# An RWKV layer on one NeuronCore: shifted inputs from a scaled copy and the neighbours' sum, GpSimd's queue in the scan, and operands at 1.7 parts per stretch

## The chip, the core and the metric

The program runs on one NeuronCore of a Trainium2 chip. The metric is device time in microseconds (us). The engines are named as in the profile: PE is TensorE (PEld its weight loads), DVE is VectorE, ACT is ScalarE, POOL is GpSimd, SP is SyncE, which issues most of the DMAs.

## What is computed

The program is a chain of blocks over 512 tokens and, from the second half on, 256 context tokens, all at width 1024: hybrid layers, a gated unit, one RWKV layer, latent attention, and a gated unit again. Only the RWKV layer is touched. Its reference, cut to what matters:

```python
def center_shift(h):
    prev = jnp.pad(h[:, :-1], ((0, 0), (1, 0), (0, 0)))
    nxt = jnp.pad(h[:, 1:], ((0, 0), (0, 1), (0, 0)))
    return 0.5 * (prev + nxt) - h

def rwkv7_features(h, mu, w_in, ...):
    xx = center_shift(h)
    xs = h[:, :, None, :] + xx[:, :, None, :] * mu          # six shifted inputs
    rkvz = jnp.einsum('blcd,cde->blce', xs[:, :, :4], w_in)  # r, k, v, z
    ...                                                      # decay w and rate a from xs[4], xs[5]

def rwkv7_scan(state0, r, decay, k_dir, v, kk, a, emit):     # two directions, 16 heads of 64
    def step(S, inp):
        s_kk = jnp.einsum('nbhvk,nbhk->nbhv', S, kk_t)
        S = S * w_t - s_kk * (kk_t * a_t) + v_t * k_t
        y_t = jnp.einsum('nbhvk,nbhk->nbhv', S, r_t)
        return S, y_t

def rwkv7_output(y, r, k_dir, v, z, r_k, ln_gain, ln_bias, w_out):
    yn = head_norm(y) * ln_gain + ln_bias
    bonus = sum(r * k_dir * r_k) * v
    return ((yn + bonus) * silu(z)) @ w_out
```

The kernel computes the scan in chunks of 64 tokens (12 chunks, context and tokens together, in each direction). For each chunk it needs products within the chunk and the inverse of a unit triangular matrix.

## The kernel before, in words

Activations lie with features on partitions: 1024 features are eight tiles of 128, and a tile has 768 columns (512 tokens, 256 context). A float32 product is made of three: each operand is split into a high part (hi, a copy on ACT) and a low part (lo, a subtraction), and `mm3` multiplies hi by hi, lo by hi and hi by lo. Weights arrive raw by DMA (wraw), ACT makes whi, and DVE or POOL makes wlo.

**features()** makes the scan's inputs. `strips()` walks over the kinds in the order k, r, z, v. A kind has eight strips, a strip is 128 output features, and a strip has eight steps of 128 input features, each with three products of two pieces (512 and 256 columns). So a strip is 24 pairs of matmuls. After every two steps, `strips()` yields: that is a stretch, four to a strip. At a yield `features()` gives each of four side jobs its credit: `lora` 1.0 parts per stretch, `operands` OPS = 2.4, `by_tokens` 2.5, `first` 3.0; beside the first and last strip of a kind, only 0.4 of these. PE's order is fixed as written here (`in_order`); the orders of the other engines come from a scheduler, except in the opening, where those of DVE and POOL are fixed too.

The opening works on the eight input tiles in a pipeline: `hidden` (norm and modulation, L1360), `neighbours` (POOL adds the left and the right neighbour into xx), `difference` (DVE turns xx into half the sum minus h, L1372), `shifted` (DVE makes xs = xx times mu plus h in two pieces, L1383; ACT copies its high part, L1384; POOL or DVE makes its low part, L1385), and then the products of two strips of k. `shifted` is called for six inputs of eight tiles: k, r, z, v and the two of `lora`. The inputs of the next kind are made beside the last strip of a kind.

`operands(f)`, for each of eight feature tiles, has 17 parts: matmuls for decay and rate (L1603), transposes by matmul (L1264), a chain of some thirty elementwise operations with two scans (L1621 to L1664), which writes st_ar and st_bk, and for either direction `within`, the chunk products of st_ar and st_bk (L1679). `by_tokens(f)` turns v of one tile to token order once its strip and its operands are done. `feature_out` for strip f of v runs the side jobs until by_tokens has reached f - 2.

`first()` starts when v's inputs are ready. It computes inverse 0 on DVE: 31 columns of two operations each (L1819, L1821). It does `merge(0)`, which makes the chunk's whole inverse from its blocks, and waits until all eight operands are done. Then it starts inverse 1 on POOL, in whose queue two DMA issues and two memsets (L1812, L1813) stand ahead of the columns.

**scan()** has nine stages p. The lanes of stage p are the first six steps of tile p and the last six of tile p - 1; a step copies rh from PE's sums on DVE (L1892), multiplies it by the inverse (L1885), and goes on to the next state. Beside the lanes are woven: the products of coming groups, `merge(p+1)`, `inverse(p+2)` on POOL, and `output(p-2)`. An output ends so: ACT scales and shifts yacc (L1957), POOL adds the bonus (L1959), DVE multiplies by z (L1961), ACT makes yh and POOL yl, and the products with the output weights follow. `merge` also clears two quarters of its tile TT, on POOL (L1846).

Of the kernel before, what the change touches and what calls it, by code (L numbers as in the profile page):

```python
# [11 lines left out]
F32 = mybir.dt.float32  # L12
# [3 lines left out]
AF = mybir.ActivationFunctionType  # L16
ALU = mybir.AluOpType
# [4 lines left out]
KD = D // 128  # L22
# [1161 lines left out]
PACE = 0.4  # L1184
OPS = 2.4
WT = 3


class Rwkv:
# [92 lines left out]
    def params_with(self, kp):  # L1282
        net, nc = self.net, self.net.nc
        with net.psum(0, 2):
            P = self.params(kp)

        self.hb = kp.tile([128, 48], F32, name="hb")
        nc.vector.tensor_scalar(self.hb[:, 0:16], P["w0"], 0.5, None, ALU.mult)
        nc.vector.tensor_scalar(self.hb[:, 16:32], P["a0"], 0.5, None, ALU.mult)
        nc.vector.tensor_scalar(self.hb[:, 32:40], P["ka"], 0.5, None, ALU.mult)  # L1290
        nc.vector.tensor_scalar(self.hb[:, 40:48], P["ka"], -0.5, 1.0, ALU.mult, ALU.add)

        self.bones = kp.tile([128, 128], F32, name="bones")
        nc.gpsimd.memset(self.bones, 0.0)
        for e in range(2):
            nc.gpsimd.memset(self.bones[64 * e:64 * e + 64, 64 * e:64 * e + 64], 1.0)
        return P
# [69 lines left out]

    def difference(self, k):

        for src, _, n, t0 in self.hp:  # L1370
            xv = self.xx[k][:, t0:t0 + n]
            self.net.nc.vector.scalar_tensor_tensor(xv, xv, 0.5, src[k], ALU.mult, ALU.subtract)  # L1372

    def shifted(self, c, k, pool, tags, eng, late=False):

        nc, T = self.net.nc, S + C
        mu = self.P["mu"][:, c * 8 + k:c * 8 + k + 1]
        n = 9 if pool is self.xsp else 1
# [3 lines left out]
        for src, _, n, t0 in self.hp:  # L1382
            nc.vector.scalar_tensor_tensor(t[:, t0:t0 + n], self.xx[k][:, t0:t0 + n], mu, src[k], ALU.mult, ALU.add)  # L1383
        nc.scalar.copy(hi, t)  # L1384
# [30 lines left out]
    def strips(self):  # L1415
# [9 lines left out]
        with in_order(net.tc, nc.vector, nc.gpsimd):  # L1425
            for j in range(KD + 4):
                for at, part in enumerate((self.hidden, self.neighbours, self.difference)):
                    if 0 <= j - at < KD:
                        part(j - at)
                if 0 <= j - 3 < KD:  # L1430
                    x, l = prep(0, j - 3, True)
                    xs.append(x)
                    low.append(l)
                if j >= 4:
                    k = j - 4
                    low[k]()
# [38 lines left out]
    def first(self):  # L1475

        tc = self.net.tc
        while self.done["xs"] != "v":
            yield
        self.cur = cur = [{} for k in range(KD)]  # L1480
        X = [self.big(2), self.big(3)]
        cut = lambda t, a, n: t[:, a:a + n]
# [349 lines left out]
    def merge(self, k, cur, work, acc):  # L1832

        net, nc, ap = self.net, self.net.nc, self.ap
        mt = cur["mt"]
        TA = cur["TT"] = work("TT", [128, 2, NS, CH], 1, k)
        T12 = work("T12", [128, 2, 24, 32], 1)
        T1, M = T12[:, 0], T12[:, 1]
        TF = TA.rearrange("p d s t -> p (d s) t")
        for e in range(2):  # L1840
            nc.sync.dma_start(M[64 * e:64 * e + 32], self.mo[k][e])
            nc.sync.dma_start(T1[64 * e:64 * e + 32], self.blocks(mt[1], e, 0))
            for h in range(2):
                q = 64 * e + 32 * h
                nc.sync.dma_start(TF[q:q + 32, :, 32 * h:32 * h + 32], self.blocks(mt[0], e, h))
            nc.gpsimd.memset(TF[64 * e + 32:64 * e + 64, :, 0:32], 0.0)  # L1846
        for _ in range(8):
# [85 lines left out]
    def output(self, k, cur):  # L1933
# [24 lines left out]
        yield  # L1958
        nc.gpsimd.tensor_tensor(y, y, bonus, ALU.add)  # L1959
        yield  # L1960
# [3 lines left out]
        yl = ap.tile([128, T], F32R, tag="yl", name="yl", bufs=1)  # L1964
        net.split(yh, yl, y, nc.gpsimd)
        yield
        for f in range(KD):
            if f % 4 == 0:
                hi, lo = net.wtile([(0, net.I["rwkv_w_out_2"][0][rows, f * 128:f * 128 + 512])], 1, 512)
            a, b = net.acc(), net.acc()  # L1970
# [492 lines left out]
```

## Time and profile before

| What | Value |
|---|---|
| Median of three runs (lowest, highest) | 4227.73 us (4226.45, 4228.69) |
| Profiled execution: its own time, its span | 4218.81 us, 4216.9 us |
| PE, PEld, busy share of the span | 91%, 76% |
| DVE, ACT, POOL, busy share of the span | 58%, 37%, 31% |
| Mean DMA rate | 102 GB/s |

The RWKV layer lies between about 1990 and 3080 us of the span. Its stages, with PE's busy time in each:

| Stage, us of the span | Length | PE busy | DVE busy | POOL busy |
|---|---|---|---|---|
| Opening, 1994 to 2045 | 51 | 26.9 | 48.6 | 35.3 |
| Strips of k, 2045 to 2125 | 80 | 79.9 | 43.5 | 25.1 |
| Strips of r and z, operands, 2125 to 2425 | 300 | 230.5 | 211.1 | 158.6 |
| Strips of v, 2425 to 2540 | 115 | 102.7 | 53.1 | 90.1 |
| First part of the scan, 2540 to 2700 | 160 | 86.7 | 63.1 | 138.5 |
| Rest of the scan, 2700 to 3080 | 380 | 320.2 | 266.6 | 93.6 |

An engine's share over the whole span hides such stages; a stage is read by what PE waits for in it. In the rows below, a time in square brackets is the idle time ahead of an instruction, with the engine and tile whose end released it.

### The profile page before, as it was taken

Reading aid. Unit: us, or ns where it says so; the run is one execution under the profiler, and the core shown is the slowest. Engines: PE = TensorE matmul, PEld = TensorE weight load, DVE = VectorE, ACT = ScalarE, POOL = GpSimd, SP = SyncE. Lnnn points to the kernel's source line nnn. Section 1 sums busy time; section 2 is a strip of 40 time slices with the busy share of each in tenths; the row PEclk is TensorE's granted clock in tenths of the full one; section 3 lists DMA queues with packets and bytes.
Section 4 is the critical chain, followed back from the end, with each engine's and each line's share of the span. In section 5 each row is a group of like instructions: output and inputs, shape, how many; then the busy total and the mean of one; then the engine's idle time right before and its main releaser. Section 6 shows DMA issues by size and latency. Waiting matters only on the chain. (4 is left out here: it accounts for less than half of the span.)

```text
span 4216.9 us, 67232 instructions
## 1 busy us (share of the span) xinstructions
PE 3855.6 (91%) x26432; PEld 3192.2 (76%) x26432; DVE 2461.7 (58%) x4804; ACT 1545.2 (37%) x2945; POOL 1317.8 (31%) x1340
## 2 busy tenths in 40 slices
PE   8999999999999999998887797588789899998999
PEld 7867777787877788887766576477577788887887
DVE  7836445865554434444767644477643778883544
ACT  4243223334332422223454433244343455553222
POOL 3321111322111211113445578820121344442221
PEclk9999999999999999999899898799889999999999
DMA  3125543213364322222257866355223121221332
GB/s 92 51 79 162 175 132 90 61 56 100 103 202 158 102 65 61 60 61 78 70 158 202 226 166 156 91 128 124 79 61 114 51 61 52 61 77 62 93 91 85
DMA packets 599015, 431.72 MB, mean 102 GB/s; under 512 B 193436, under 2 KB 532140, under 8 KB 598700
## 3 DMA queue, kind: packets, MB, share of 16 engines
q1 hardware_dynamic: 593756, 414.97, 34.1%
q0 software_dynamic: 4944, 12.46, 1.2%
q8 instruction: 209, 3.42, 0.3%
q14 instruction: 106, 0.87, 0.1%
HBM read 354.46 MB, written 68.68 MB: 100 GB/s over the span
## 5 line engine op out<-in xcount | busy, mean ns | idle before, releaser
L138 ACT CAST whi<-wraw 128x1024 fp32r<-128x1024 f32 (+3 forms) x471 | 457.5, 972 | 1183.0 <-PE acc L160 971.4
L141 POOL TENSOR_TENSOR wlo<-wraw,whi 128x1024 fp32r<-128x1024 f32 (+2 forms) x205 | 426.9, 2083 | 1291.3 <-ACT whi L138 1182.1
L160 PE MATMUL acc<-hh,whi 128*128 128x512 f32 (+2 forms) x1776 | 625.2, 377 | 9.5 <-ACT hh L421 5.0
L160 PE MATMUL acc<-hl,whi 128*128 128x512 f32 (+2 forms) x1776 | 620.8, 374 | 2.5 <-DVE hl L422 2.5
L160 PE MATMUL acc<-hh,wlo 128*128 128x512 f32 (+2 forms) x1776 | 620.3, 374 | 2.0 <-DVE wlo L141 2.0
L141 DVE TENSOR_TENSOR wlo<-wraw,whi 128x1024 fp32r<-128x1024 f32 (+3 forms) x266 | 330.6, 1244 | 467.1 <-ACT whi L138 420.7
L160 PEld LDWEIGHTS acc<-hh,whi 128*128 128x128 f32 (+1 forms) x1776 | 314.7, 188 | 84.0 <-ACT whi L138 17.3
L160 PEld LDWEIGHTS acc<-hh,wlo 128*128 128x128 f32 (+1 forms) x1776 | 314.4, 187 | 63.4 <-DVE wlo L141 2.8
L160 PEld LDWEIGHTS acc<-hl,whi 128*128 128x128 f32 (+1 forms) x1776 | 314.6, 188 | 62.3 <-DVE hl L422 4.1
L160 PE MATMUL acc<-wlo,hh 128*128 128x256 f32 (+1 forms) x896 | 297.2, 332 | 6.5 <-DVE wlo L141 6.5
L160 PE MATMUL acc<-whi,hh 128*128 128x256 f32 (+1 forms) x896 | 298.1, 335 | 2.9 <-ACT hh L978 2.3
L160 PE MATMUL acc<-whi,hl 128*128 128x256 f32 (+1 forms) x896 | 293.4, 331 | 1.5 <-DVE hl L979 1.5
L999 DVE SCALAR_TENSOR_TENSOR xT<-acc,mod,xT 128x512 f32<-128x512 f32 x256 | 185.6, 746 | 139.6 <-PE acc L160 138.9
L160 PEld LDWEIGHTS acc<-wlo,hh 128*128 128x128 f32 x896 | 179.5, 201 | 20.4 <-DVE wlo L141 7.3
L160 PEld LDWEIGHTS acc<-whi,hh 128*128 128x128 f32 x896 | 179.4, 201 | 20.5 <-ACT hh L978 2.9
L160 PEld LDWEIGHTS acc<-whi,hl 128*128 128x128 f32 x896 | 178.4, 200 | 16.3 <-DVE hl L979 2.4
L160 PE MATMUL wide<-xsh,whi 128*128 128x512 f32 (+1 forms) x512 | 147.4, 371 | 16.5 <-ACT xsh L1384 16.5
L160 PE MATMUL wide<-xsl,whi 128*128 128x512 f32 (+1 forms) x512 | 142.0, 360 | 17.0 <-POOL xsl L1385 13.5
L160 PE MATMUL wide<-xsh,wlo 128*128 128x512 f32 (+1 forms) x512 | 140.0, 356 | 0.0
L160 PE MATMUL acc<-ffgh,whi 128*128 128x512 f32 x352 | 139.9, 400 | 0.0
L160 PE MATMUL acc<-ffgl,whi 128*128 128x512 f32 x352 | 138.4, 395 | 0.0
L160 PE MATMUL acc<-ffgh,wlo 128*128 128x512 f32 x352 | 138.3, 395 | 0.0
(625 smaller groups left out, 8754.9 us busy)
## 6 DMA issues: line engine op xcount, KB each, us to landing
ada_w<-in_ada_w SPq DMA_DIRECT2D x32, 1536.0 KB
wraw<-in_sgu_w_in SPq DMA_DIRECT2D x96, 512.0 KB
wraw<-in_w_up SPq DMA_DIRECT2D x88, 512.0 KB
wraw<-in_w_in SPq DMA_DIRECT2D x44, 512.0 KB
wraw<-in_w_down SPq DMA_DIRECT2D x32, 512.0 KB
wraw<-in_sgu_w_out SPq DMA_DIRECT2D x32, 512.0 KB
wraw<-in_rwkv_w_in SPq DMA_DIRECT2D x32, 512.0 KB
bk<-rw_bk SPq DMA_DIRECT2D x24, 512.0 KB
```

What stands on the lines that cost most here:

```text
L138: nc.scalar.copy(hi, raw)
L141: eng.tensor_tensor(lo, raw, hi.bitcast(F32), ALU.subtract)
L160: mm(out, lhsT=a, rhs=b[:, t0:t1], start=first and n == 0, stop=last and n == 2)
L999: nc.vector.scalar_tensor_tensor(dst[k], ps, m[:, 16 + k, j:j + 1], dst[k], ALU.mult, ALU.add)
```

## The change

Four edits, all in the RWKV layer.

1. The shifted input is written as (1 - mu) h plus mu/2 times the neighbours' sum. `difference` is gone; for each shifted input ACT makes two scaled copies of h (512 and 256 columns), and DVE adds the sum in one operation of 768 columns. Two tables of factors, mus, are made once. The opening's pipeline is one tile shorter.
2. OPS is 1.7 instead of 2.4.
3. In an output, the bonus add, and the low part yl, go from POOL to DVE, and so does wlo of the output weights, of which the third in turn was POOL's.
4. TT has three tiles that stay, instead of one for each merge from a pool, and they are cleared by DVE in the first three merges only.

The inverse itself is as it was; it stays on POOL.

```diff
-OPS = 2.4
+OPS = 1.7
...
+        self.mus = kp.tile([128, 2, 48], F32, name="mus", bufs=1)
+        nc.vector.tensor_scalar(self.mus[:, 0], P["mu"], -1.0, 1.0, ALU.mult, ALU.add)
+        nc.vector.tensor_scalar(self.mus[:, 1], P["mu"], 0.5, None, ALU.mult)
...
-    def difference(self, k):
-
-        for src, _, n, t0 in self.hp:
-            xv = self.xx[k][:, t0:t0 + n]
-            self.net.nc.vector.scalar_tensor_tensor(xv, xv, 0.5, src[k], ALU.mult, ALU.subtract)
...
         for src, _, n, t0 in self.hp:
-            nc.vector.scalar_tensor_tensor(t[:, t0:t0 + n], self.xx[k][:, t0:t0 + n], mu, src[k], ALU.mult, ALU.add)
+            nc.scalar.activation(t[:, t0:t0 + n], src[k], AF.Copy, scale=mu[:, 0])
+        nc.vector.scalar_tensor_tensor(t, self.xx[k], mu[:, 1], t, ALU.mult, ALU.add)
         nc.scalar.copy(hi, t)
...
-            for j in range(KD + 4):
-                for at, part in enumerate((self.hidden, self.neighbours, self.difference)):
+            for j in range(KD + 3):
+                for at, part in enumerate((self.hidden, self.neighbours)):
...
-        TA = cur["TT"] = work("TT", [128, 2, NS, CH], 1, k)
+
+        if k < 3:
+            self.tts.append(work("TT", [128, 2, NS, CH], 1, k))
+        TA = cur["TT"] = self.tts[k % 3]
...
-            nc.gpsimd.memset(TF[64 * e + 32:64 * e + 64, :, 0:32], 0.0)
+            if k < 3:
+                nc.vector.memset(TF[64 * e + 32:64 * e + 64, :, 0:32], 0.0)
...
-        nc.gpsimd.tensor_tensor(y, y, bonus, ALU.add)
+        nc.vector.tensor_tensor(y, y, bonus, ALU.add)
...
-        net.split(yh, yl, y, nc.gpsimd)
+        net.split(yh, yl, y)
...
-                hi, lo = net.wtile([(0, net.I["rwkv_w_out_2"][0][rows, f * 128:f * 128 + 512])], 1, 512)
+                hi, lo = net.wtile([(0, net.I["rwkv_w_out_2"][0][rows, f * 128:f * 128 + 512])], 1, 512, nc_lo=nc.vector)
```

How the order of instructions moves, at three places. A line number is that of the kernel the rows belong to.

DVE in the opening, two tiles of the pipeline. L1360 (L1364 after) is `hidden`, xx_16291 (xx_16294) the neighbours' sum, xT and cT the tiles of tokens and context. Before:

```order
L1360 SCALAR_TENSOR_TENSOR xT_81<-xT_81,mod_4351,aux 128x512
L1360 SCALAR_TENSOR_TENSOR cT_11756<-cT_11756,mod_4351,aux 128x256
L1372 SCALAR_TENSOR_TENSOR xx_16292<-xx_16292,xT_79 128x512
L1372 SCALAR_TENSOR_TENSOR xx_16292<-xx_16292,cT_11754 128x256
L1383 SCALAR_TENSOR_TENSOR xs<-xx_16291,col_rwkv,xT_78 128x512
L1383 SCALAR_TENSOR_TENSOR xs<-xx_16291,col_rwkv,cT_11753 128x256
```

After:

```order
L1382 SCALAR_TENSOR_TENSOR xs<-xx_16294,mus,xs 128x768
L1364 SCALAR_TENSOR_TENSOR xT_81<-xT_81,mod_4351,aux 128x512
L1364 SCALAR_TENSOR_TENSOR cT_11756<-cT_11756,mod_4351,aux 128x256
L1382 SCALAR_TENSOR_TENSOR xs<-xx_16295,mus,xs 128x768
L1364 SCALAR_TENSOR_TENSOR xT_82<-xT_82,mod_4351,aux 128x512
```

Four operations of DVE for a tile's shifted input have become one, which reads the scaled copy (xs) that ACT made.

PE at the last of the `within` products (L1679). Before, in strip 5 of z; wide_19399 is that strip's sum:

```order
L160 MATMUL wide_19399<-xsh_18370,wlo_19396 128x512
L160 MATMUL wide_19399<-xsh_18370,wlo_19396 128x256
L1679 MATMUL aux_19473<-st_ar_19450,st_bk_19451 64x64 [waits DVE_49]
L1679 MATMUL aux_19473<-st_ar_19450,st_bk_19451 64x64 x15
L1679 MATMUL aux_19491<-st_ar_19450,st_bk_19451 64x64 [waits Activation_49]
L1679 MATMUL aux_19491<-st_ar_19450,st_bk_19451 64x64 x7
L160 MATMUL wide_19399<-xsh_18383,whi_19395 128x512
```

After, in strip 4 of v; wide_20032 is its sum, L1553 belongs to `by_tokens`, L1870 to merge 0:

```order
L160 MATMUL wide_20032<-xsh_19285,wlo_20029 128x512
L160 MATMUL wide_20032<-xsh_19285,wlo_20029 128x256
L1679 MATMUL aux_20194<-st_ar_20122,st_bk_20123 64x64 [waits DVE_49,Activation_49]
L1679 MATMUL aux_20194<-st_ar_20122,st_bk_20123 64x64 x15
L1679 MATMUL aux_20212<-st_ar_20122,st_bk_20123 64x64 [waits Activation_49]
L1679 MATMUL aux_20212<-st_ar_20122,st_bk_20123 64x64 x7
L1553 MATMUL aux_20228<-vt_20048,back_19471 128x128 [waits PE_49,Activation_49]
L1870 MATMUL aux_20236<-xx3_19949,xx2_19948 32x32 [waits PE_49,Activation_49]
L160 MATMUL wide_20032<-xsh_19299,whi_20028 128x512
```

The last operand has moved by seven strips, past the change of kind, and now stands among the token passes and merge 0.

POOL at the first output of the scan, among the columns of an inverse. Before:

```order
L1819 TENSOR_TENSOR invP<-invA,invT 96x240
L1959 TENSOR_TENSOR yacc<-yacc,ld_b 128x768
L1821 TENSOR_TENSOR invT<-invT,invP 96x12x20
L1819 TENSOR_TENSOR invP<-invA,invT 96x231
L1821 TENSOR_TENSOR invT<-invT,invP 96x11x21
L178 TENSOR_TENSOR yl<-yacc,yh 128x768
```

And DVE at the same output after, where L1896 is the copy of rh, L1963 the bonus add, L1965 the multiplication by z:

```order
L1896 COPY rh<-aux 128x128 x2
L1959 TENSOR_TENSOR yacc<-yacc,acc 128x512
L1959 TENSOR_TENSOR yacc<-yacc,acc 128x256
L1902 COPY VU<-aux 64x2x64
L1963 TENSOR_TENSOR yacc<-yacc,ld_b 128x768
L1902 COPY VU<-aux 64x2x64
L1912 SCALAR_TENSOR_TENSOR st<-st,rw_ec,aux 128x64 x2
L1965 SCALAR_TENSOR_TENSOR yacc<-yacc,ld_z 128x768
```

The add and the low part have left POOL's inverse columns; the add now stands in DVE's queue between two copies of a step.

## Rows read from the trace of the kernel before

**Rows 1.** Stretches: us, busy (count) of PE, PEld, DVE, ACT, POOL; PEclk, DMA, GB/s

```profile
1994.00:2045.00 51.00, 26.91 (x103) 20.63 (x101) 48.58 (x56) 19.65 (x30) 35.29 (x24) 0.66 0.14 34
...
2125.00:2425.00 300.00, 230.45 (x1748) 184.50 (x1746) 211.12 (x180) 147.27 (x220) 158.63 (x103) 0.90 0.74 203
2425.00:2540.00 115.00, 102.66 (x771) 86.33 (x770) 53.11 (x93) 34.00 (x61) 90.08 (x149) 0.94 0.62 172
```

**Rows 2.** PE's waits in 2125 to 2425 us: sum, count, longest

```profile
PE aux L1679 <- DVE st_bk L1647: 40.6, 13, 5.6
```

**Rows 3.** PE's timeline: start, us, operation, [idle before, releaser]; operands and strips

```profile
2140.20 1.87 PE L1603 MATMUL aux<-hw,w 64*128 64x512 f32 x8
...
2197.90 1.56 PE L1603 MATMUL aux<-hw,w 64*128 64x512 f32 x8
...
2205.09 0.66 PE L1264 MATMUL aux<-ident,hs_rep 128*128 128x128 f32 x4 [1.82 <-ACT tmp L1604]
...
2209.20 0.51 PE L160 MATMUL wide<-xsl,whi 128*128 128x512 f32 x2
2209.55 0.51 PE L160 MATMUL wide<-xsh,wlo 128*128 128x512 f32 x2
...
2217.74 1.61 PE L1679 MATMUL aux<-st_ar,st_bk 64*64 64x64 f32 x48 [3.45 <-DVE st_bk L1647]
...
2226.12 2.78 PE L1679 MATMUL aux<-st_ar,st_bk 64*64 64x64 f32 x48 [2.33 <-DVE st_bk L1647]
...
2391.86 1.61 PE L1679 MATMUL aux<-st_ar,st_bk 64*64 64x64 f32 x48 [3.19 <-DVE st_bk L1647]
```

**Rows 4.** Timelines of ACT, DVE and PE at the scan's first output

```profile
2647.00 1.03 ACT L1957 ACTIVATE yacc<-yacc,col_rwkv 128x768 f32<-128x768 f32 x1 [0.25 <-DVE yacc L1955]
...
2693.61 1.43 DVE L1961 SCALAR_TENSOR_TENSOR yacc<-yacc,ld_z 128x768 f32<-128x768 f32 x1 [43.12 <-POOL yacc L1959]
...
2695.30 1.12 PE L1885 MATMUL aux<-rh,xx 64*64 64x64 f32 x16 [44.29 <-DVE rh L1892]
```

**Rows 5.** POOL's timeline: the bonus adds of the third and fourth outputs

```profile
2808.51 1.82 POOL L1959 TENSOR_TENSOR yacc<-yacc,ld_b 128x768 f32<-128x768 f32 x1 [17.10 <-ACT yacc L1957]
...
2861.81 1.82 POOL L1959 TENSOR_TENSOR yacc<-yacc,ld_b 128x768 f32<-128x768 f32 x1 [16.55 <-ACT yacc L1957]
```

**Rows 6.** Lines L1372, L1383 by form: count: least/median/longest ns, first to last us

```profile
L1372 DVE SCALAR_TENSOR_TENSOR xx<-xx,xT x8: 677/680/1523, 2001.0 to 2033.9; 128x512 f32<-128x512 f32 x8
L1372 DVE SCALAR_TENSOR_TENSOR xx<-xx,cT x8: 411/621/2032, 2002.5 to 2034.5; 128x256 f32<-128x256 f32 x8
...
L1383 DVE SCALAR_TENSOR_TENSOR xs<-xx,col_rwkv,xT x48: 736/752/2430, 2008.0 to 2423.1; 128x512 f32<-128x512 f32 x48
L1383 DVE SCALAR_TENSOR_TENSOR xs<-xx,col_rwkv,cT x48: 469/478/2780, 2008.6 to 2423.8; 128x256 f32<-128x256 f32 x48
```

**Rows 7.** Timelines: end of DVE's inverse, the scan's first product, its first merge product

```profile
2468.57 0.19 DVE L1821 TENSOR_TENSOR xx<-xx,xx 96x31 f32<-96x31 f32 x1
...
2539.46 0.45 PE L1885 MATMUL aux<-SV,G 128*64 128x64 f32 x8
...
2571.34 1.06 PE L1854 MATMUL acc<-xx 32*32 32x32 f32 x32
```

**Rows 8.** DVE's groups, 2125 to 2425 us: busy, mean ns | idle before, releasers

```profile
L1625 DVE TENSOR_TENSOR_SCAN tmp<-rreset,tmp 128x768 f32<-128x768 bf16 x16 | 28.8, 1843 | 34.8 <-ACT tmp L1621 34.8
...
L1646 DVE TENSOR_TENSOR st_ar<-eb,ld_r 128x768 f32<-128x768 f32 x16 | 22.0, 1373 | 11.4 <-PE aux L1679 5.0 <-DMA ld_r<-rw_r 4.0 <-ACT kd L1617 1.2
```

**Rows 9.** POOL's timeline: first memset of inverse 1; ends of two inverses

```profile
2406.46 0.96 POOL L1812 MEMSET invT<- 96x1024 f32 x1 [4.15 <-DMA rw_mo<-tmp]
...
2575.29 1.94 POOL L1825 TENSOR_SCALAR invA<-invT 96x1024 f32<-96x1024 f32 x1
...
2618.55 1.94 POOL L1825 TENSOR_SCALAR invA<-invT 96x1024 f32<-96x1024 f32 x1
```

**Rows 10.** Line L1385, low parts of shifted inputs: least/median/longest ns

```profile
L1385 POOL TENSOR_TENSOR xsl<-xs,xsh x32: 1801/1844/2706, 2010.0 to 2426.2; 128x768 fp32r<-128x768 f32 x32
L1385 DVE TENSOR_TENSOR xsl<-xs,xsh x16: 944/954/2602, 2024.4 to 2421.1; 128x768 fp32r<-128x768 f32 x16
```

## What the time will be, and why

> **What bounds the kernel now.** TensorE is busy for nine tenths of the span, so I first looked for the stages in which it is not. The busy times by stretch show them between 1994 and 2700 us, all inside the RWKV layer, in three places.
>
> First, the opening (1994 to 2045 us): TensorE has 27 us of work in 51, VectorE 48.6 [rows 1]. VectorE is the bound there.
>
> Second, the strips of r and z (2125 to 2425 us): TensorE works 230 of 300 us, at a mean granted clock of 0.90, with the DMA engines 0.74 busy [rows 1]. The waits of TensorE say for what: 40.6 us in 13 waits for the operand tile st_bk that the matmuls of `within` read [rows 2]. TensorE's own order is fixed there, so everything behind such a matmul waits too. The rows of one operand show the chain: it begins at 2197.90, its transposes wait 1.82 us, its two `within` products wait 3.45 and 2.33 us [rows 3]. The eight operands run from 2140.20 to about 2393.5, 31.7 us each [rows 3]. The v strips after them (2425 to 2540 us) run at 102.7 busy of 115 [rows 1].
>
> Third, the scan: the bonus add of the first output is queued on GpSimd among the column steps of an inverse. Its input is ready at 2648.03, when ScalarE ends, but VectorE gets the sum at 2693.61 after 43.12 us of idleness, and TensorE sits idle for 44.29 us behind VectorE's copy of rh [rows 4]. Later outputs follow each other in 53.3 us [rows 5]. Had the first add run on time, the one at 2808.51 would have run at 2648.0 + 2 x 53.3 = 2754.6: the stall costs 53.9 us with its slow restart.
>
> **The change part by part.** The sum is made against the profiled execution, 4218.8 us; the median of the runs is 8.9 us above it.
>
> *Start.* The differences go: 8 x (0.68 + 0.62) = 10.4 us of VectorE [rows 6]. Each shifted input becomes one operation on 768 columns instead of 0.752 + 0.478; on the line through these two it takes about 1.0 (an estimate), so 8 save 1.8. ScalarE takes two copies more for each, some 1.2 us for both (an estimate from its 1.03 us for 768 columns in one piece [rows 4]); it works 19.7 of the 51 us there [rows 1], so this hides until VectorE waits for it. Removed from the bound: 12 us. What is late next is GpSimd's chain of sums and low parts, and TensorE's own 16 products of 8 steps. I take -9, between 0 (GpSimd was the true bound) and -12.
>
> *Strips.* The chain of an operand stays as long as it is; what changes is how much strip work lies inside it. A pair of matmuls follows the last one in 0.35 us [rows 3], so a strip of 24 pairs costs 8.4 us. It has four stretches. At 2.4 parts per stretch the 17 parts of an operand span 1.77 strips, or 14.9 us; its own products are 2 x 1.56, 2 x 1.61 and about 0.7, together 7.0. That makes 21.9 us of work in 31.7, so 9.8 us is lost, some 5.1 of it at st_bk (40.6 / 8) and 2 at the transposes. At 1.7 parts an operand spans 2.5 strips: 21.0 + 7.0 = 28.0 us. By the order about two more stretches (4.2 us) stand between products and their readers, so I keep 3.5 us of the waits, and 1.5 for clock and changes of kind: 33 us. From r's first strip (2116, being 2125 less the 9 above) the 16 strips of r and z with the 5.3 operands in them take 16 x 8.4 + 5.3 x (7.0 + 5.0) = 198, and about 10 for the change of kind: they end near 2324.
>
> The other 2.7 operands now fall into v's strips 0 to 4, beside the inverse that VectorE computes. That ended at 2468.8, 44 us after v began, with little else on VectorE [rows 7]. The five costliest VectorE operations of an operand took 28.8 to 22.0 us for eight operands [rows 8], about 127 us in all or 15.9 per operand, 18 with the small ones: 44 + 2.7 x 18 = 92 us of VectorE against some 75 of TensorE. So the last `within` comes at about 2324 + 93 = 2417. The remaining 3.3 strips and token passes at 114.5 / 8 = 14.3 us each [rows 1] plus a drain give 55 us. The scan begins at 2472, not at 2539.46 [rows 7]: -67 with the start, -58 alone. Bounds: operands at 40 us, which put the scan's start at 2503, leave -27; operands at the old 31.7 us and nothing lost in v give -93.
>
> *Inverses.* They now wait for the last operand. GpSimd's first memset came at 2406.46, 13 us after the last `within` [rows 9]; so the first starts near 2430. One cycle is 43.3 us (2575.29 to 2618.55) [rows 9], and the last weight split costs 2.4 more: the first inverse is out at 2476. In the scan the first merge product stands 31.9 us after the start (2539.46 to 2571.34) [rows 7], now 2504. That leaves 28 us for two stores and six loads. Each later stage takes longer than an inverse, so GpSimd gains ground. I cost this at nothing; the cover is those 28 us.
>
> *Stall.* The bonus add goes to VectorE at 0.95 us, the price of the same shape there, instead of 1.84 [rows 10]. In VectorE's queue it waits for ScalarE's scaling and for the load of the bonus; behind it stand the copies of the scan's steps, for which TensorE waits, but they stood behind the multiplication by z at the same place before. -54, between -44 (only the wait) and -60.
>
> *Steady scan.* VectorE gets about 0.95 + 0.95 + a third of a weight split, some 2.2 us per stage, while the chain of an output gets shorter by twice 0.9 us. I set these against each other. But the 53.3 us were measured with GpSimd idle [rows 5], and four stages will now run beside inverses: wide VectorE operations take up to three times as long beside GpSimd (0.752 against 2.430) [rows 6]. A few such operations per stage at half a microsecond: +6 in all, from -5 to +14. The memsets of TT (three merges instead of eight) and the two columns of factors cost under 2 us, hidden behind TensorE.
>
> The Trainium skill ("SBUF — State Buffer", section "SBUF: two separate sides") speaks against this step: a VectorE operation with two SBUF inputs and a GpSimd operation that reads SBUF exclude each other for a whole instruction. The rows 0.736 against 2.430 agree in kind. By that rule alone each of three moved operations in five outputs could wait for one inverse step of 0.7 us: +10 instead of +6.
>
> Sum: -9 - 58 - 54 + 6 = -115; 4218.8 - 115 = 4103.8, and 4113 on the scale of the medians.
>
> **The rivals.** *Operands keep their pace.* If 31.7 us per operand was latency alone, the last `within` comes at 2385, the scan at 2437: 4078. For it: the chain's links are ScalarE, VectorE and GpSimd, less loaded per time. Against: TensorE's work alone is 28, and VectorE's inverse lies in the same stretch.
>
> *Operands slow down.* With VectorE and the DMA engines shared by strips, tokens and operands to the end, 40 us each: 2131 + 320 + 52 = 2503 for the scan's start: 4144. For it: a DMA share of 0.74 already; against: the load is spread over a longer time.
>
> *GpSimd takes over the start of the scan.* If the first inverse starts 20 us later and a cycle takes 48, stages 0 to 2 wait for the merges about 25 us: 4138.
>
> *Slower: the inverse chain becomes the scan's clock.* All seven inverses now begin after the operands, at 2430. The seventh is needed one stage before the output whose add ran at 2808.5 + 3 x 53.3 = 2968. With some 48 us for merge and output, this is later than before once a cycle exceeds (2968 - 48 - 2430) / 7 = 70 us instead of 43.3; at 75 it gives 4228 + 35 = 4263. For it: wide operations do collide. Against: an inverse cycle beside the scan's VectorE work is the measured one.
>
> *The change does nothing.* The add's wait returns as another (for its load, say), and the operands take 50 us each: about 4225. Nothing in the rows points to it.
>
> **How the numbers follow.** Forecast 0.50 (4095 to 4130), old pace 0.16, slow operands 0.17, GpSimd late 0.09, nothing 0.03, slower 0.05. The range leaves out the last two and the outermost part of the first rivals: all bounds at their good end give 4058, all at their bad end 4171; I take 4070 to 4178, a little less than all the good luck at once and a little more than the bad. Within 0.2% is 8.5 us, about what a measurement of this kernel can tell from no change: faster 0.92, the same 0.03, slower 0.05.
>
> **What would show it.** In the profile after: the first hidden-to-first-strip stretch some 9 us shorter; waits for st_bk below 30 us over a longer stretch; operands about 33 us apart; the last `within` near 2417; the scan's first product near 2472; no wait of tens of microseconds for yacc; outputs 53 to 55 us apart from the second on. The forecast is wrong if operands are over 40 us apart, if TensorE waits long for a merge in stages 0 to 2, or if outputs come more than 57 us apart.

## The result and the profile after

The changed kernel takes 4152.97 us (median of four runs, 4150.81 to 4162.26); the kernel before, with one run more beside it, 4227.09. The ratio is 0.983 with a 95% interval of 0.9814 to 0.9849. The forecast was 4113 us, a gain of 115 us; the gain is 74. The time lies in the stated range (4070 to 4178), but above the 4095 to 4130 that had been given half the chance.

Stages are compared from the layer's first row on, the matmul L251 on rs at 1992.41 us before and 1987.82 us after, because the part ahead of it differs by itself (last section). "Opening and k" ends where ScalarE starts to copy the last strip of k, "r and z" where it starts on the last strip of z, "v" at the scan's first product, and "scan" at the start of the last bonus add. All times in us; the experiments are told below.

| Kernel | Median | Opening and k | r and z | v | Scan | Layer |
|---|---|---|---|---|---|---|
| before | 4227.1 | 130.8 | 283.9 | 132.4 | 513.0 | 1060.0 |
| after | 4153.0 | 123.0 | 243.0 | 161.5 | 471.2 | 998.6 |
| e1_scan_only | 4176.8 | 130.6 | 289.0 | 137.4 | 463.5 | 1020.5 |
| e2_ops_only | 4197.7 | 132.2 | 245.4 | 155.6 | 515.2 | 1048.4 |
| e3_shift_only | 4206.4 | 123.0 | 284.7 | 134.4 | 507.2 | 1049.3 |
| e4_ops_back | 4159.9 | 123.0 | 284.0 | 131.4 | 467.8 | 1006.2 |
| e5_bonus_only | 4215.9 | 132.2 | 284.1 | 128.4 | 513.2 | 1057.9 |
| e6_short_inverse | 4150.3 | 121.4 | 245.1 | 159.0 | 469.0 | 994.7 |
| e7_ops_20 | 4164.8 | 122.9 | 277.3 | 138.2 | 471.0 | 1009.4 |
| e8_ops_14 | 4200.7 | 122.9 | 235.9 | 183.1 | 509.3 | 1051.2 |
| e9_first_short | 4157.8 | 123.0 | 244.5 | 158.3 | 484.0 | 1009.7 |
| e10_within_free | 4207.8 | 130.6 | 275.1 | 129.6 | 515.2 | 1050.5 |
| e11_low_parts | 4146.3 | 121.1 | 235.3 | 158.4 | 474.4 | 989.3 |
| e12_m_tile | 4142.8 | 122.6 | 232.8 | 165.7 | 470.5 | 991.8 |

A stage that no edit touched differs by up to 6 us between profiles (r and z of before, e1 and e5: 283.9, 289.0, 284.1; the scan of before and e3: 513.0, 507.2); smaller differences of one stage are not read. Beside the experiments the kernel before had medians of 4220.2 to 4222.9 us, not 4227.1, and each ratio below is against its own of these. So medians of the table are compared through the ratios: an experiment whose median is some 6 us below that of after need not be faster.

Of the 61.4 us that the layer lost, 7.8 are in the opening and k, 40.9 in r and z, 41.8 in the scan, and v gave 29.1 back. Now the busy times, in the columns of [rows 1]: the opening up to the end of k's first strip, r and z, v, and the first 160 us of the scan. Before, cut at the same places:

```profile
1992.40:2044.95 52.55, 28.50 (x108) 22.23 (x108) 48.53 (x56) 19.60 (x30) 35.29 (x24) 0.66 0.18 39
2123.20:2407.10 283.90, 220.97 (x1725) 178.48 (x1724) 200.78 (x171) 144.66 (x218) 145.12 (x86) 0.91 0.73 199
2407.10:2539.50 132.40, 113.53 (x798) 93.65 (x797) 64.75 (x102) 37.98 (x66) 103.37 (x166) 0.91 0.66 183
2539.50:2699.50 160.00, 86.62 (x1605) 73.80 (x1604) 63.14 (x197) 41.13 (x136) 138.54 (x249) 0.72 0.50 118
```

After:

```profile
1987.80:2030.90 43.10, 25.85 (x108) 20.61 (x108) 29.19 (x31) 29.85 (x49) 34.68 (x24) 0.71 0.22 49
2110.80:2353.75 242.95, 204.96 (x1495) 165.65 (x1495) 161.48 (x130) 134.91 (x206) 115.40 (x65) 0.92 0.68 189
2353.75:2515.20 161.45, 131.22 (x1024) 105.45 (x1023) 87.07 (x130) 66.86 (x116) 90.41 (x111) 0.89 0.75 206
2515.20:2675.20 160.00, 128.19 (x2316) 110.27 (x2318) 91.66 (x296) 57.04 (x184) 133.89 (x243) 0.78 0.67 148
```

In the opening VectorE falls from 48.5 to 29.2 us and ScalarE rises from 19.6 to 29.9; 9.5 us are won. In the scan TensorE does 128 us of work in 160 instead of 87. The two middle rows are the ones to look at: **TensorE's busy time over r, z and v together is 334.5 us before and 336.2 after.** At a granted clock that hardly changed (0.91 and 0.91, then 0.92 and 0.89), what could be won there was its idle time alone, 81.8 us before, and 68.2 of it are left. TensorE's waits in r and z (sum, count, longest) answer to [rows 2]:

```profile
PE aux L1264 <- ACT tmp L1604: 15.1, 8, 4.2
PE wide L160 <- POOL xsl L1384: 6.6, 6, 1.6
PE aux L1679 <- DVE st_bk L1647: 5.6, 5, 2.0
PE wide L160 <- ACT xsh L1383: 3.8, 3, 2.2
PE aux L1679 <- DVE st_ar L1649: 3.2, 1, 3.2
```

Before, in the same stage:

```profile
PE aux L1264 <- ACT tmp L1604: 15.9, 11, 3.7
PE wide L160 <- POOL xsl L1385: 2.2, 2, 1.3
```

The 40.6 us for st_bk have become 5.6. But the transposes wait as long as before for six operands instead of eight, and the shifted inputs of the next kind are waited for (6.6 + 3.8 us). In v small waits of twelve kinds stand, none over 4.2 us; the longest:

```profile
PE aux L1858 <- DMA xx<-rw_mt: 4.2, 1, 4.2
PE aux L1555 <- DVE rst L1565: 3.6, 1, 3.6
PE aux L1264 <- ACT tmp L1604: 3.3, 2, 1.7
```

The first products of operands 0, 2, 3, 5 and 6 (of 0 to 7), and the last `within` (to [rows 3]):

```profile
2128.98 1.56 PE L1603 MATMUL aux<-hw,w 64*128 64x512 f32 x8
...
2195.16 1.56 PE L1603 MATMUL aux<-hw,w 64*128 64x512 f32 x8
...
2243.85 1.56 PE L1603 MATMUL aux<-hw,w 64*128 64x512 f32 x8
...
2314.70 1.56 PE L1603 MATMUL aux<-hw,w 64*128 64x512 f32 x8
...
2355.98 1.81 PE L1603 MATMUL aux<-hw,w 64*128 64x512 f32 x8
...
2448.52 1.61 PE L1679 MATMUL aux<-st_ar,st_bk 64*64 64x64 f32 x48
```

From one operand's first product to the next one's it takes 32.9, 33.3, 48.7, 33.2, 37.6, 41.3 and 49.1 us: two intervals inside r, one across the change to z, two inside z, one across the change to v, one in v. From the first product to the end of the last `within`, over eight operands, it is 40.1 us for each, where the kernel before has 31.7.

Last, the scan: the first memset of an inverse on GpSimd and the end of that inverse (to [rows 9]), the scan's first product and its first merge (to [rows 7]), and ScalarE's scaling and four bonus adds, now VectorE's (to [rows 4, 5]).

```profile
2457.86 0.97 POOL L1812 MEMSET invT<- 96x1024 f32 x1
...
2506.34 1.99 POOL L1825 TENSOR_SCALAR invA<-invT 96x1024 f32<-96x1024 f32 x1
...
2515.22 0.69 PE L1889 MATMUL aux<-SV,G 128*64 128x64 f32 x8 [3.55 <-ACT vb L1556]
...
2546.89 1.06 PE L1858 MATMUL acc<-xx 32*32 32x32 f32 x32
...
2625.00 1.03 ACT L1961 ACTIVATE yacc<-yacc,col_rwkv 128x768 f32<-128x768 f32 x1 [0.32 <-DVE yacc L1959]
...
2626.06 0.96 DVE L1963 TENSOR_TENSOR yacc<-yacc,ld_b 128x768 f32<-128x768 f32 x1 [0.83 <-ACT yacc L1961]
...
2682.26 1.14 DVE L1963 TENSOR_TENSOR yacc<-yacc,ld_b 128x768 f32<-128x768 f32 x1 [0.83 <-ACT yacc L1961]
...
2738.42 1.12 DVE L1963 TENSOR_TENSOR yacc<-yacc,ld_b 128x768 f32<-128x768 f32 x1 [0.83 <-ACT yacc L1961]
...
2795.94 0.96 DVE L1963 TENSOR_TENSOR yacc<-yacc,ld_b 128x768 f32<-128x768 f32 x1 [0.83 <-ACT yacc L1961]
```

The add runs 1.06 us after ScalarE began the scaling, every time; the 43 us of [rows 4] are gone. The adds follow each other in 56.2, 56.2 and 57.5 us, the next two in 53.3 and 53.6.

A stall of the same kind is left in the scan, in VectorE's queue. The low part wlo of the output weights waits there for ScalarE's whi, and the copy of rh that TensorE needs stands behind it:

```profile
2541.70 0.69 DVE L141 TENSOR_TENSOR wlo<-wraw,whi 128x512 fp32r<-128x512 f32 x1 [9.21 <-ACT whi L138]
...
2543.30 0.69 PE L1889 MATMUL aux<-rh,xx 64*64 64x64 f32 x8 [10.39 <-DVE rh L1896]
```

The kernel before has it too, with 8.1 us of TensorE's idle time ahead of the product at 2567.76; this wlo is VectorE's in both kernels.

### The profile page after: what moved, and what is told of

It reads as the page before. It is cut to its first block, busy times and chain, and to the rows that moved or that the text cites. A ratio compares the mean times of both kernels' runs of the same rounds, so it can differ in the third digit from the quotient of the medians.

```text
span 4148.8 us, 67237 instructions
## 1 busy us (share of the span) xinstructions
PE 3856.5 (93%) x26432; PEld 3194.9 (77%) x26432; DVE 2427.8 (59%) x4769; ACT 1592.1 (38%) x3041; POOL 1270.4 (31%) x1303
## 5 line engine op out<-in xcount | busy, mean ns | idle before, releaser
L141 POOL TENSOR_TENSOR wlo<-wraw,whi 128x1024 fp32r<-128x1024 f32 (+2 forms) x200 | 418.2, 2091 | 1246.9 <-ACT whi L138 1139.4
L999 DVE SCALAR_TENSOR_TENSOR xT<-acc,mod,xT 128x512 f32<-128x512 f32 x256 | 185.6, 746 | 127.6 <-PE acc L160 126.8
L160 PEld LDWEIGHTS acc<-whi,hl 128*128 128x128 f32 x896 | 178.1, 199 | 14.3 <-issue 0.8
L160 PE MATMUL wide<-xsh,whi 128*128 128x512 f32 (+1 forms) x512 | 148.2, 373 | 14.7 <-ACT xsh L1383 13.7
L160 PE MATMUL wide<-xsl,whi 128*128 128x512 f32 (+1 forms) x512 | 142.8, 362 | 18.7 <-POOL xsl L1384 16.0
```

The lines of the kernel that those rows point to most:

```text
L141: eng.tensor_tensor(lo, raw, hi.bitcast(F32), ALU.subtract)
L160: mm(out, lhsT=a, rhs=b[:, t0:t1], start=first and n == 0, stop=last and n == 2)
L999: nc.vector.scalar_tensor_tensor(dst[k], ps, m[:, 16 + k, j:j + 1], dst[k], ALU.mult, ALU.add)
```

## The experiments

### One part of the change at a time

e1: the scan's edits alone, in the kernel before (the third and fourth of the change; the lines on TT and on the output weights' wlo are as in the whole diff).

```diff
...
-        nc.gpsimd.tensor_tensor(y, y, bonus, ALU.add)
+        nc.vector.tensor_tensor(y, y, bonus, ALU.add)
...
-        net.split(yh, yl, y, nc.gpsimd)
+        net.split(yh, yl, y)
...
```

> The kernel before with the scan's edits alone: bonus add, low part yl, wlo of the output weights on VectorE, TT in three tiles cleared by VectorE. Theory A (the stall behind the bonus add is a cost by itself, and steady outputs beside inverses cost a little): the 44 us wait at the first output is gone, outputs come 53 to 57 us apart from the first, 4227 - 42 to -52, that is 4175 to 4185 us. Rival (the inverses must first be ahead or behind in the way the whole change sets them): the wait returns for a merge or another tile, over 4210 us.

Measured: 4176.83 us, ratio 0.9892 (0.9877 to 0.9906). The scan takes 463.5 us instead of 513.0, with its first outputs 56.2 and 57.0 us apart. Theory A.

e2: the number of parts alone.

```diff
-OPS = 2.4
+OPS = 1.7
```

> The kernel before with OPS 1.7 alone. Theory A (slower operands save about 12 us of TensorE's idle time before the scan, but start the first POOL inverse some 50 us later, so that the bonus add, still in GpSimd's queue among the columns, comes later too): the scan starts near 2527, the first bonus add near 2715 instead of 2691.8, in all 4230 to 4255 us, slower than before. Rival (the strips' gain is independent of the rest): 4227 - 12 = 4215 us. Rival of the prediction (58 us from the strips): 4169 us.

Measured: 4197.69 us, ratio 0.9944 (0.9929 to 0.9959): neither theory's time. The strips did what the changed kernel's do (r and z 245.4, v 155.6, together 15.3 us less). The scan did not get longer by much (515.2), since the first add stands earlier among the columns, in the fifth of GpSimd's inverses and not in the sixth, but the stall stays and is spread over two outputs: the first add waits, and the second comes 67.3 us after it. VectorE's multiplication by z behind the first add:

```profile
2661.15 1.33 DVE L1961 SCALAR_TENSOR_TENSOR yacc<-yacc,ld_z 128x768 f32<-128x768 f32 x1 [26.86 <-POOL yacc L1959]
```

Of the 24 to 29 us by which the medians differ, the layer explains 11.6; the rest lies in parts that no edit touched.

e3: the shifted inputs alone (mus, `shifted`, the opening's loop; the diff ahead of the prediction has it).

> The kernel before with the new shifted inputs alone. Theory A (the opening is bound by VectorE): the first strip of k ends 12 to 14 us earlier, the rest is moved with it, 4213 to 4217 us; the copies beside the kinds' last strips load ScalarE and take back at most 3. Rival (the strips of r and z are bound by chains that run over ScalarE, which now has 48 x 2 more copies): under 6 us left, 4221 us or more.

Measured: 4206.41 us, ratio 0.9962 (0.9948 to 0.9977). Opening and k take 123.0 us instead of 130.8, exactly as after, and r and z keep their length, 284.7. The first strip of k ends 9.5 us earlier, not theory A's 12 to 14, and the layer is 10.7 us shorter, more than the rival's 6: nearer to theory A, by the stages. The median is 15.5 us below that of the kernel before beside it, some 5 better than the layer.

e4: the changed kernel with the old OPS.

```diff
-OPS = 1.7
+OPS = 2.4
```

> The changed kernel with OPS 2.4 again. Theory A (operands at 1.7 parts were worth about 12 us of the strips): scan starts near 2527 instead of 2515, 4160 to 4168 us. Rival (the 12 us hide a gain of r and z that v takes back, and without it the inverses start earlier and the scan's first outputs are not beside them): 4150 us or less. Prediction's reading (58 us from the strips): 4199 us or more.

Measured: 4159.86 us, ratio 0.9847 (0.9831 to 0.9864) against the kernel before. The layer is 7.6 us longer than after: r and z 41 us longer, v 30 shorter, the scan 3 shorter. Theory A by the stages (the scan starts 538.4 us after the layer's first row, after 527.4); the time is at the lower edge of its range, and the ratio's interval overlaps that of the whole change. The parts add up: e1, e2 and e3 shorten the layer by 39.5, 11.6 and 10.7 us, together 61.8; the whole change by 61.4.

### The stall in GpSimd's queue

e5: the first diff line of e1 alone; the low part yl stays on GpSimd.

> The kernel before with the bonus add alone on VectorE; the low part yl, the output weights' wlo and TT's clearing stay on GpSimd. Theory A (whatever of an output is left in GpSimd's queue among the inverse columns stalls TensorE in the same way, since TensorE's order is fixed): the wait moves from yacc to yl, the first output's products start 30 to 45 us late, and at most 15 us are won, 4208 us or more. Rival (the add was the one operation that the scan waited for, since the copies of rh stood behind it): as with all the scan's edits, 4177 to 4183 us.

Measured: 4215.94 us, ratio 0.9992 (0.9983 to 1.0002). The first add runs on time, 113.1 us after the scan's start, and the second comes 102.3 us after it. TensorE, behind the low part:

```profile
2700.02 1.01 PE L160 MATMUL acc<-yl,whi 128*128 128x512 f32 x2 [43.33 <-POOL yl L178]
```

The wait is as long as before and has only changed its name. Theory A: the add and the low part have to leave GpSimd's queue together. Whether the weights' wlo and TT's clearing had to go too was not tried by itself.

### What the inverses cost the scan

e6: the changed kernel with short inverses on GpSimd.

```diff
-        for j in range(31):
+        for j in range(31 if k < 2 else 1):
```

> The changed kernel with the GpSimd inverses of tiles 2 to 7 cut to their first column of 31, so that GpSimd is nearly idle in the scan (it leaves out those columns). Theory A (the first outputs come 56.2, 56.2 and 57.5 us apart, and not 53.5, because GpSimd's inverses run beside VectorE's work): they come 53 to 54 us apart, the layer gets 8 to 10 us shorter, 4143 to 4146 us. Rival (the early stages are longer by their own work, clears, loads and merges): spacing as it was, 4150 to 4155 us.

Measured: 4150.30 us, ratio 0.9824 (0.981 to 0.9839). The first outputs come 54.2, 53.2 and 54.7 us apart, together 7.8 us less than after. But the first add came 3.5 us later and the two adds behind these three 2.1 later in all, so the scan is only 2.2 us shorter, and the layer 3.9. Theory A is right in the spacing; its 8 to 10 us of the layer did not come, and the median lies in the rival's range. The spacing has a witness in e1: 57.0 us while inverses run, and 53.2 once the last of them has ended at 2758 us. VectorE's groups from 2515 to 2800 us (busy, mean ns | idle before) show what GpSimd takes. After:

```profile
L1919 DVE TENSOR_TENSOR SV<-st,rw_ec 64x128 f32<-64x128 f32 x54 | 19.1, 366 | 1.5
L999 DVE SCALAR_TENSOR_TENSOR xT<-acc,mod,xT 128x512 f32<-128x512 f32 x24 | 18.0, 749 | 14.8 <-PE acc L160 14.4
...
L178 DVE TENSOR_TENSOR yl<-yacc,yh 128x768 fp32r<-128x768 f32 x4 | 4.4, 1110 | 0.1
```

With GpSimd nearly idle:

```profile
L999 DVE SCALAR_TENSOR_TENSOR xT<-acc,mod,xT 128x512 f32<-128x512 f32 x24 | 18.0, 748 | 15.1 <-PE acc L160 14.7
...
L1919 DVE TENSOR_TENSOR SV<-st,rw_ec 64x128 f32<-64x128 f32 x53 | 14.7, 289 | 1.5
...
L178 DVE TENSOR_TENSOR yl<-yacc,yh 128x768 fp32r<-128x768 f32 x3 | 2.9, 958 | 0.1
```

### What the strips can give

e7 and e8: OPS 2.0 and 1.4 in the changed kernel.

> The changed kernel with OPS 2.0. Theory A (what r and z win per operand moved, v gives back but for the waits for st_bk): between OPS 2.4 and 1.7, the scan's first product 534 us after the layer's first rows (527 at 1.7, 538 at 2.4), 4155 to 4158 us. Rival (an optimum between, where r and z have their waits covered and v has only one operand): 522 us or less, 4148 or less.

> The changed kernel with OPS 1.4. Theory A (work is only moved; the operands that land in v are forced there without strip work between, and GpSimd's first inverse starts later still): r and z 15 to 20 us shorter, v 25 to 35 longer, the scan's first product 8 to 15 us later than at 1.7, 4160 to 4170 us. Rival (the waits go on falling with the parts per stretch): 4145 us or less.

Measured: 4164.82 us, ratio 0.9862 (0.9846 to 0.9879), and 4200.71 us, ratio 0.9951 (0.9934 to 0.9967). At 2.0 the scan starts 538.4 us after the layer's first row, not 534: no better than at 2.4. At 1.4 r and z lose only 7 us more (theory A: 15 to 20), v grows by 22 (theory A: 25 to 35), and the scan starts 14.5 us later than at 1.7, within theory A's 8 to 15. The time is far above its range all the same, because GpSimd ends its first inverse (the operation of L1825) 27 us after the scan's start, where after it does so 8.9 us ahead of it: the first add comes 143.0 us into the scan instead of 110.8. TensorE's three long waits before it:

```profile
2565.56 0.28 PE L1858 MATMUL acc<-xx 32*32 32x32 f32 x2 [9.89 <-DMA xx<-rw_mt]
...
2617.63 0.79 PE L1774 MATMUL acc<-G,bk 64*128 64x128 f32 x2 [19.48 <-DMA G<-rw_ar]
...
2659.87 0.79 PE L1774 MATMUL acc<-G,bk 64*128 64x128 f32 x2 [11.13 <-DMA G<-rw_ar]
```

The first waits for the load of the first inverse. The two others wait for loads of G that SyncE issued at 2610.82 and 2655.63, behind the loads of the second and the third inverse, for whose stores its queue had stood still 22.1 and 9.9 us. The busy times of r and z and of v at 1.4:

```profile
2109.70:2345.60 235.90, 196.21 (x1337) 157.17 (x1335) 154.54 (x117) 121.96 (x186) 103.08 (x57) 0.90 0.63 172
2345.60:2528.70 183.10, 140.34 (x1184) 111.61 (x1185) 103.90 (x142) 78.35 (x137) 76.74 (x68) 0.87 0.77 206
```

TensorE's work is 336.6 us once more, and now 82.4 are idle. That 1.4 is worse than the three others is shown. Among 2.4, 2.0 and 1.7 the lowest ratio is that of 1.7 (0.9847, 0.9862, 0.9831), but the intervals overlap; the layers, one profile each, are 1006.2, 1009.4 and 998.6 us.

e10: the kernel before, with `within` on a constant tile.

```diff
-lhsT=bk[hf[e], c, 0], rhs=ar[hf[e], c, 0],
+lhsT=self.bones[hf[e], 64 - 64 * e:128 - 64 * e], rhs=self.bones[hf[e], 64 - 64 * e:128 - 64 * e],
```

> The kernel before (OPS 2.4) with the chunk products of the operands reading a constant tile of zeros instead of st_ar and st_bk, so that TensorE never waits for these two, 40.6 us in the strips of r and z (it leaves the chunk products' values out). Theory A (a wait of TensorE for an operand is only the place where it meets the pace of the operand's chain; without it, it meets it at the products for decay and rate and at the transposes): r and z get 10 to 25 us shorter, the waits for tmp rise from 20 to over 30 us. Rival (each wait is a delay by itself, and taking it away gives all of it): 35 to 45 us shorter, the other waits as they were.

Measured: 4207.77 us, ratio 0.9972 (0.9961 to 0.9982). All 40.6 us of waits for st_bk are taken away, and r and z get 8.8 us shorter. TensorE's waits there:

```profile
PE aux L1264 <- ACT tmp L1604: 14.4, 10, 3.7
PE aux L1603 <- ACT tmp L1680: 14.4, 5, 4.7
PE wide L160 <- DVE rst L1522: 4.7, 2, 4.4
PE aux L1603 <- ACT tmp L1604: 4.4, 3, 2.5
```

The waits at tmp are 33.2 us instead of 19.9, and 4.7 us at rst are new. TensorE's idle time in the stage fell by 14.7 us (62.9 to 48.2), and its busy time rose by 5.9, at a granted clock of 0.89 instead of 0.91. Theory A, a little beyond its range: the wait for st_bk was for the greater part a place where TensorE met the pace of the operand's chain, and without it they meet at another product.

e9: the changed kernel with inverse 0 short on VectorE (the edit of e6, for tile 0 alone).

> The changed kernel with inverse 0, which VectorE computes beside the strips of v, cut to its first column of 31 (it leaves out the others). Theory A (what v took back of the gain is VectorE's inverse, 56 us long, in the way of two operands' chains): v's stretch from the last strip of z to the scan's first product falls from 161 to 148 us or less, 4140 us or less. Theory B (v took back TensorE's own work of two operands and their transposes' waits, whatever VectorE does beside): 157 to 162 us, 4148 to 4154.

Measured: 4157.78 us, ratio 0.9845 (0.983 to 0.9859), some 4 us above theory B's range and 18 above theory A's. VectorE's busy time in v falls by a quarter, and v from 161.5 to 158.3 us:

```profile
2359.50:2517.70 158.20, 127.84 (x1026) 103.27 (x1024) 65.00 (x70) 66.03 (x115) 83.16 (x102) 0.89 0.75 206
```

The last `within` starts 91.3 us after z, in the changed kernel 94.8. Theory B by the stage: VectorE's inverse beside the strips of v did not cost the gain. The scan took 12.8 us more than after, its first outputs 58 to 63 us apart; the schedule behind the cut differs, and the reason stays open.

### Two attempts at what is left

e11: half of the low parts of the shifted inputs on VectorE.

```diff
-nc.vector if k % 3 == 2 else nc.gpsimd, late)
+nc.vector if k % 2 else nc.gpsimd, late)
```

> The changed kernel with half of the low parts of the shifted inputs on VectorE instead of a third (0.95 us there, 1.84 us on GpSimd). Theory A (the waits for xsl, 16 us from the opening to the scan, which came up when those for st_bk went, are GpSimd's pace): they fall below 8 us and the scan's first product comes 4 to 8 us earlier, 4145 to 4150 us. Rival (they are the place where TensorE meets VectorE's and ScalarE's shifted inputs, whoever makes the low part): the waits stay above 12 us in sum, or move to xsh, 4151 to 4156 us.

Measured: 4146.28 us, ratio 0.9821 (0.9804 to 0.9839). r and z take 235.3 us, and the scan starts 12.5 us earlier than after, more than theory A said; but the waits for xsl fell from 18.7 us only to 14.3: those for GpSimd's low parts from 16.0 to 5.6, while those for VectorE's rose from 2.7 to 8.7. The sum is the rival's, so theory A's mechanism is shown for a part at best.

e12: on top of e11, a tile of its own for the chunk products of operands 0 to 4.

```diff
-        M, hf = tmp(), (slice(0, 64), slice(64, 128))
+        M, hf = tmp() if f > 4 else self.ap.tile([128, S + C], F32, tag="vt", name="vt", bufs=1), (slice(0, 64), slice(64, 128))
```

> The kernel of e11_low_parts with a tile of its own for the chunk products M of operands 0 to 4, instead of one of the four tmp tiles, which ScalarE otherwise takes over for the next operand only when M's stores have landed (20 us of ScalarE's waits for tmp in the strips of r and z). Theory A (that ring of four tiles sets the operands' pace there, and the transposes' waits for tmp, 11 to 15 us, come from it): ScalarE's wait goes, the transposes' waits halve, r and z fall from 235 to 222 to 229 us, 4134 to 4142 us. Rival (the chain over ScalarE, VectorE and GpSimd sets the pace and the ring only shows where it is met, as st_bk did): the wait goes but r and z stay within 4 us of 235, 4143 to 4149 us.

Measured: 4142.84 us (five runs), ratio 0.982 (0.9807 to 0.9834). ScalarE's 20 us of waits for tmp on a store are gone (10.2 come back at the new tile), but TensorE's waits barely moved:

```profile
PE aux L1264 <- ACT tmp L1604: 11.6, 9, 3.4
PE aux L1679 <- DVE st_bk L1647: 10.0, 6, 3.3
```

r and z take 232.8 us, within 4 of e11. The rival: the ring of tiles is again only a place where the chain's pace is met. e11 and e12 have the lowest medians here, but their ratios (0.9821, 0.982) are only 0.001 below that of after (0.9831), and the three intervals overlap: that they beat it is not shown.

## Why the prediction was right or wrong, step by step

**Start: right.** -9 us was forecast. The opening up to k's first strip is 9.5 us shorter, and 7.8 are left at the end of k; e3 has the same. VectorE lost more than the sum's 12 us there, 19.3 (48.5 to 29.2): the differences alone took 14.5, not 10.4, since the medians of [rows 6] pass over the operations that took two or three times as long. It gave 9.5 us all the same: something else is late next, as the prediction said, and what it is was not tried.

**Strips: the step that failed.** -58 us was forecast, -11.9 measured (r and z -40.9, v +29.1). TensorE's groups of the operands in r and z after (busy, mean ns | idle before):

```profile
L1679 PE MATMUL aux<-st_ar,st_bk 64*64 64x64 f32 x576 | 22.8, 242 | 8.9 <-DVE st_bk L1647 5.6 <-DVE st_ar L1649 3.2
L1603 PE MATMUL aux<-ha,a 64*128 64x512 f32 (+1 forms) x48 | 11.5, 516 | 1.1 <-ACT tmp L1604 1.1
L1603 PE MATMUL aux<-hw,w 64*128 64x512 f32 (+1 forms) x48 | 9.4, 509 | 0.0
L1264 PE MATMUL aux<-ident,hs_rep 128*128 128x128 f32 x36 | 7.0, 334 | 15.1 <-ACT tmp L1604 15.1
```

The pieces, as the prediction put them:

- Operands about 33 us apart was right for three intervals only (32.9, 33.3 and 33.2 us). The four others are 37.6 to 49.1 us, and counted as the 31.7 of the kernel before was, an operand takes 40.1. The sum had 1.5 us for an operand's clock and changes of kind and some 10 for the change to z. The longest intervals in r and z lie across the changes of kind, where `features()` gives operands 0.4 of their parts; that this is their cause is argued from the program, and no run changed that factor. Waits for st_bk below 30 us was right: 5.6.
- The end of z was put at 2324 and came at 2353.75: 243 us instead of 208. Twelve chunk products stand in r and z, which is six operands, not 5.3. Their work is 50.7 us, 8.5 for each: the price of the sum (7.0 and 1.5). Too small was the strip. The stretch's 205 us of work less these 50.7 and 2.6 for the key sums leave 152, or 9.5 us for each of sixteen strips, not 8.4; in the kernel before it was 9.2 by the same working. The 8.4 came from a pair that follows the last one in 0.35 us. The mean granted clock was 0.92, hardly more than the 0.91 before, so the spells at 1.2 GHz still cost up to (1 - 0.92) x 243 = 19 us of the stretch, which I had put at 8. And idle time is 38 us, not 5.3 x 3.5 + 10 = 28.6. So the 35 us are 17 for the strips, 6 for the operands, 3 for the key sums and 9 of idle time.
- v was put at 148 us and took 161.5. The last `within` came 94.8 us after z, as forecast (93), but that was luck: 44 of the 93 us were VectorE's inverse, and in e9, which leaves out all but one of its columns, the last `within` still comes 91.3 us after z. The rest took 66.7 us instead of 55. By the trace the last `within` has moved by six strips, from strip 6 of z (counted from 0) to strip 4 of v, and not by seven.

Behind the pieces is one error: r and z were credited with 76 us (284 to 208) for the 2.7 operands that leave, 28 us for each and near their whole pitch of 31.7, and v was charged 16 us for taking them in. TensorE's work did not leave, so only idle time could, and -58 would have left 24 of 82 us of it. The rows in [rows 1] held both sums. e10 shows why the idle time is tough: taking away 40.6 us of named waits gave 8.8.

**Inverses: right.** The first was forecast out at 2476, 28 us ahead of the first merge. It came out at 2508, and the merge ran 38 us later; both had moved with the scan's start. Its cost was nothing, as said. e8 shows the rival that was feared, one step further on: there the first inverse is late, and the first output 32 us later.

**Stall and steady scan: right, with a larger price for the contention.** -54 and +6 make -48; measured -41.8 from the scan's start to the last add. Without a stall and at 53.3 us the third add would have come 106.6 us after the first; it came 112.4 after it, and the fourth 10.0 late in all. e6 ties 7.8 us of this spacing to GpSimd's inverses, though the scan as a whole got only 2.2 us of it back. The prediction put the stall down to the bonus add alone; that was too narrow, and the stall went only because the change moves yl too: e5 shows that yl alone stalls as long.

**The sum.** The layer gave 61.4 us where 115 was forecast: 46 us missing in the strips, 6 in the scan, 1 at the start. The rival that came nearest is the one of slow operands: 40 us for each, the last `within` at 2451, the scan at 2503 and 4144 in all, where 40.1, 2450, 2515 and 4153 were measured. Its reason is not shown. It named VectorE and the DMA engines, shared to the end; in e9, without VectorE's inverse, an operand still takes 39.9 us, and the DMA engines' share was not tested. Two of the prediction's own signs of being wrong are met: operands over 40 us apart, and one output 57.5 us behind the last. The other 13 us of the measured 74 lie outside the layer and were forecast by no term. In the two profiles 4.6 of them are ahead of it and 2.1 behind; the remaining 6 are that the profiled executions lie 8.3 us (before) and 2.2 us (after) below their medians.

## What to carry to other kernels

Before a wait is counted as a gain, add up the bound engine's work over all stages that the edit moves work between: only the idle part can be won, and most of a wait taken away at one instruction can come back at the next one that meets the same chain (here 40.6 us gave 8.8). When an in-order engine waits for one operation in a long queue, move everything that the consumer needs from that queue, not the first name in the profile. A rate that spreads side work over a main loop can be too low: here 1.4 parts per stretch made the work that spills past the loop cost more than the waits it covered. A price per piece is taken from the whole stage (9.2 us for a strip), not from the best row in it (8.4), and a pitch from all its intervals.

## What was not expected of the hardware

Beside GpSimd's inverses VectorE's operations on two SBUF tiles got slower and those with one operand in PSUM did not: SV took 366 ns instead of 289 (mean), yl 1110 instead of 958, while L999, which reads acc from PSUM, took 749 and 748. The Trainium skill, "SBUF — State Buffer", section "SBUF: two separate sides", has such an exclusion between a VectorE operation with two SBUF inputs and a GpSimd operation that reads SBUF; these rows agree in kind. The kernel before shows it too: of its 112 operations of L1372 and L1383, each on two SBUF tiles, 26 took over 1 us, and all 26 ran beside a GpSimd operation; of the 86 others 23 did.

The part of the program ahead of the layer, whose instructions stand in the same order in both kernels on TensorE, ScalarE and GpSimd (VectorE has two operations on mus more and four swaps of neighbours), took 1992.4 us before, 1987.8 after, and between 1985.6 and 1995.9 in the twelve other profiles, without relation to the edits. A gain below 0.2% can't be read from one profile's span, and why the parts outside the layer differ is not explained by these runs.
